# DeltaNet scan: the output of a half-step summed in PSUM on ScalarE-scaled values, with three PSUM banks for the scan and one for the preparation

## The chip, the core and the metric

The kernel runs on one core of a Trainium2 chip. The metric is the device time of one execution in microseconds (us). The kernel before was timed three times: 2514.2, 2525.34 and 2525.86 us, median 2525.34 us. A separate execution was profiled; it took 2514.53 us.

The engines are named as the profile names them: PE (TensorE; PEld is its weight load), DVE (VectorE), ACT (ScalarE), POOL (GpSimd) and SP (the queue that issues DMAs). Each runs its own list of instructions in order; they meet through semaphores only.

## What is computed

The reference is a two-layer diffusion transformer: layer 0 has a gated DeltaNet mixer in both time directions, layer 1 a gated linear attention; each is followed by a feed-forward net. The change touches the DeltaNet mixer alone. Cut to one head and one direction, a chunk does this:

```
decay = exp(where(tri, gcum_i - gcum_j, -inf))
m     = where(strict, beta_i * (k k^T) * decay, 0)
u, w  = solve(I + m, [v * beta, k * beta * exp(gcum)])
v_new = u - w @ s
o     = (q * exp(gcum)) @ s + ((q k^T) * decay) @ v_new
s     = s * exp(gcum_last) + (k * tail)^T @ v_new
```

`s` is the state that goes from chunk to chunk. There are 16 value heads in 8 groups of two, and both directions are added at the end: `o` forward plus `o` backward.

## The kernel before, in words

Tokens (256 of context, 512 of image) stand in 6 chunks of 128. The mixer is one long interleaved program. A Python loop over the groups g makes one *iteration* after another; in each it takes one step of three generators in turn: the scan `seq(g)`, the dense projections `stream()` and the side work (`advance()`).

- `stream()` gives one k-step an iteration: six matmuls of 128x128 weights against 256 and 512 columns. A projection is 8 k-steps and lands in a PSUM bank `d` for 512 columns and a half bank for 256. When it ends, ScalarE copies it out (`rp`), and a convolution of five taps runs on VectorE (`cv`, `tn`).
- `prep(g)` prepares a group: `dec` makes the decay factors E in a PSUM bank (PE, then exponentials on ACT); the products of K with K and with Q go to another bank; VectorE builds N and A; then VectorE eliminates 32x32 blocks in a loop of 30 steps (`tmp`, `X`), transposes the result (`Z`), and PE multiplies the blocks together (`ZM`, `LC`), which gives Y. One group's preparation is made while the scan of an earlier one runs.
- `seq(g)` is the scan: 12 half-steps h, direction d = h % 2, chunk c = order[d][h // 2]. A half-step takes three iterations. In the first, PE multiplies K and Q with the state S into one bank, here called **p1** (256 columns K·S, 256 columns Q·S, line 737); VectorE makes R from K·S (line 742); then `kx` ends the half-step before. Two iterations later PE multiplies U with R into a second bank, **p2** (line 758), and ScalarE copies that to x (`xv`, line 760). `kx` (line 702), called in the next half-step, multiplies x with Kt into p2's first half (from which VectorE updates S, line 717) and with A into p2's second half, which VectorE subtracts from the output oN (line 723).
- The share of Q·S in the output goes from p1 to oN separately: in a half-step that is the first to reach its chunk, ScalarE writes it scaled (line 748); otherwise VectorE multiplies and adds it (line 750).
- `onorm(g)` normalises the output after the scan. It ends with transposes on PE into the one bank `n` and a multiply on VectorE from it (`of`), four times, with one iteration between them (line 802).

PSUM has 8 banks. `psm(tag)` (line 111) hands them out: two `d`, one for the half-width outputs, one `n`, two `c` (the preparation) and two `s` (p1 and p2 of the scan, the K products, and the 256-column half of every second z projection). A new tile of a tag waits on PE until its bank has been read. The order of the matmuls that the generators issue is pinned to the program; the other engines' instructions are placed by a scheduler at compile time. Everything after the mixer (output projection, feed-forward, layer 1) is dense work that the change does not touch.

Of the kernel before, what the change touches and what calls it, by code (L numbers as in the profile page):

```python
# [8 lines left out]
F32 = mybir.dt.float32  # L9
# [6 lines left out]
P = 128  # L16
# [3 lines left out]
NCH = 6  # L20
# [40 lines left out]
class Dev:  # L61
# [8 lines left out]
    def nm(self, s):  # L70
        self.n += 1
        return f"{s}{self.n}"
# [4 lines left out]
    def stt(self, o, a, s, b, op0, op1):  # L77
        self.dve.scalar_tensor_tensor(o, a, s, b, op0=op0, op1=op1)  # L78
# [6 lines left out]
def body(tc, I, O):  # L85
# [3 lines left out]
    with ExitStack() as top:  # L89
# [21 lines left out]
        def psm(tag="c"):  # L111
            if PS["nc"] == 4 and PS["pair"] is None:
                tag = "c"
            return PS["c"].tile([P, 512], F32, name=nm(tag), tag=tag, bufs={"c": PS["nc"], "n": 1, "s": 2}[tag])

# [170 lines left out]
        with ExitStack() as dn:  # L286
            ps_scope(dn, True, 2)
            dc = dn.enter_context(tc.tile_pool(reuse_waits="tile", name="dc", bufs=1))

            RA = dc.tile([P, NT], F32R, name="RA")  # L290
            biasE = dc.tile([P, NCH, 2, 16], F32, name="biasE")
            neG = dc.tile([P, NCH, 2, 16], F32, name="neG")
            tailb = dc.tile([P, NCH, 2, 16], F32, name="tailb")
            eGl = dc.tile([P, NCH, 2, 16], F32, name="eGl")

            with tc.tile_pool(reuse_waits="tile", name="x0", bufs=1) as x0p, tc.tile_pool(reuse_waits="tile", name="n3", bufs=3) as n3:
# [37 lines left out]
            nc.sync.dma_start(convw, I["convw"])  # L334
            dve.tensor_scalar(dng, dng, -0.5, None, op0=MUL)

            with tc.tile_pool(reuse_waits="tile", name="gt", bufs=1) as gt:
# [34 lines left out]
                tt(biasE, Lb, Gc, SUB)  # L372
                act.activation(neG, Gc, AF.Exp)
                dve.tensor_scalar(neG, neG, -1.0, None, op0=MUL)
                ps = psm("n")
# [49 lines left out]
            def conv(ft, outs, bite, done):  # L425
                rp = rps[0]
                act.copy(rp[:, 2:258], outs[0])  # L427
                act.copy(rp[:, 260:772], outs[1])
                state["evac"] += 1
                cv = cv3.tile([P, NG], F32, name=nm("cv"), tag="c3")  # L430
                w = convw[:, ft]
                act.activation(cv, rp[:, 2:772], AF.Copy, scale=w[:, 2:3])  # L432
                yield
                for n, tap in enumerate((0, 1, 3, 4)):
                    stt(cv, rp[:, tap:tap + NG], w[:, tap:tap + 1], cv, MUL, ADD)
                    if n % bite == bite - 1:
                        yield
                t = cv3.tile([P, NG], F32, name=nm("tn"), tag="c3")
                act.activation(t, cv, AF.Tanh, scale=0.5)
                yield  # L440
                yield from done(cv, t)
# [84 lines left out]
            def prep(g, xb):  # L526
# [4 lines left out]
                def dec(c0, hh):  # L531
                    E = ehp.tile([P, 2, 2, P], F32, name=nm("E"), tag="eh")
                    ps = psm()
                    for d in range(2):
                        r = 32 * d + 2 * g + hh
                        pmm(ps[:, d * n:(d + 1) * n], selR[:, r:r + 1].broadcast_to([P, P]), RA[:, c0 * P:c0 * P + n], stop=False)
                        pmm(ps[:, d * n:(d + 1) * n], identR, mbR[d].unsqueeze(1).broadcast_to([P, 2, P]), start=False)
                    for d in range(2):
                        for c in range(2):
                            act.activation(E[:, d, c, :], ps[:, d * n + c * P:d * n + (c + 1) * P], AF.Exp,  # L540
                                           bias=biasE[:, c0 + c, d, 2 * g + hh:2 * g + hh + 1])
                    return E
# [112 lines left out]
                for dst, t in ((Nf, 0), (Y, 1)):  # L655
                    for b6 in range(2):
                        ps = psm()
                        for p_ in range(6):
                            pmm(ps[:, p_ * 64:(p_ + 1) * 64], Nf[:, 6 * b6 + p_], LC[:, t, 6 * b6 + p_])
                        pv = ps[:, 0:384].rearrange("p (s i) -> p s i", s=6)  # L660
                        act.copy(dst[hf[0], 6 * b6:6 * b6 + 6, 64:128], pv[hf[0]])
                        act.copy(dst[hf[1], 6 * b6:6 * b6 + 6, 0:64], pv[hf[1]])
                        yield
                    yield
# [8 lines left out]
            def seq(g):  # L673
# [27 lines left out]

                def kx(h, p2, x, Kt):
                    step, d = divmod(h, 2)
# [4 lines left out]
                    for hh in range(2):  # L708
                        pmm(p2[:, 256 + hh * P:256 + (hh + 1) * P], As[c // 2][:, c % 2, 2 * d + hh, :], x[:, hh])
                    if step < 5:  # L710
# [7 lines left out]
                    if not done[c]:  # L718
                        done[c] = True
                        if step == 0:  # L720
                            act.activation(oN[:, c], h2(p2[:, 256:512]), AF.Copy, scale=-1.0)
                            return
                    tt(oN[:, c], oN[:, c], h2(p2[:, 256:512]), SUB)

                nx = pre(0)
                prev = None
                for h in range(12):
                    step, d = divmod(h, 2)
                    c = order[d][step]
                    ks = slice(cg(c), cg(c) + P)  # L730
                    U, Kt = nx
                    if step == 0:
                        R = Vn[:, c]
                    else:
                        p1 = psm("s")
                        pmm(p1[:, 0:256], KT[:, ks], S[d])
                        pmm(p1[:, 256:512], QT[:, ks], S[d])
                        R = sp.tile([P, 2, P], F32, name=nm("R"), tag="R", bufs=1)
                        for hh in range(2):
                            stt(R[:, hh], p1[:, hh * P:(hh + 1) * P], neG[:, c, d, r0 + hh:r0 + hh + 1], Vn[:, c, hh], MUL, ADD)  # L740
                    if prev is not None:
                        kx(*prev)
                    if step > 0:
                        for hh in range(2):
                            pq = p1[:, 256 + hh * P:256 + (hh + 1) * P]
                            sg = neG[:, c, d, r0 + hh:r0 + hh + 1]
                            if not done[c]:
                                act.activation(oN[:, c, hh], pq, AF.Copy, scale=sg)
                            else:
                                stt(oN[:, c, hh], pq, sg, oN[:, c, hh], MUL, ADD)  # L750
                    if h == 11:
# [7 lines left out]
                    x = sp.tile([P, 2, P], F32, name=nm("xv"), tag="xv", bufs=1)  # L759
                    act.copy(x, h2(p2[:, 0:256]))  # L760
                    prev = (h, p2, x, Kt)
                    yield
# [3 lines left out]
            def onorm(g):  # L766
# [29 lines left out]
                for hh in range(2):  # L796
# [4 lines left out]
                    for c0, cn in ((0, 4), (4, 2)):  # L801
                        yield
                        ps = psm("n")
# [508 lines left out]
```

## Time and profile before

| | |
|---|---|
| profiled execution | 2514.53 us, of which the span from first to last instruction is 2512.8 us |
| median of three runs | 2525.34 us (2514.2 to 2525.86) |
| busy in the span | PE 91%, PEld 78%, DVE 63%, ACT 44%, POOL 39% |
| mean granted TensorE clock | 0.954 |
| scans of the 8 groups | first U matmuls at 219.5, 335.1, 467.5, 587.8, 702.2, 819.3, 934.3 and 1033.7 us |

The mixer's interleaved part lies between about 70 and 1110 us. What stands before is the first norm and the modulation weights; what follows to 2512.8 us is dense. The busy shares are means over all of it, so what the change is worth must be read from the stretches between 207 and 1110 us.

### The profile page before, as it was taken

What the parts mean: (1) busy time and instruction counts of PE and PEld (TensorE: products, weight loads), DVE (VectorE), ACT (ScalarE), POOL (GpSimd) and SP (SyncE); (2) the same over time, 40 slices, a digit from 0 to 9 for tenths busy, and PEclk for the clock granted to TensorE, in tenths of its full rate; (3) what the DMA queues carried; (4) which work ended last, traced back from release to release, by engine and by line L of the source; (5) the groups of instructions that cost most, each with busy time, mean ns of one, the idle gap of its engine ahead of it and who ended that gap; (6) DMA issues with size and microseconds to landing.
All of it is one profiled execution on the core that took longest, in us unless ns stands there. A gap on an engine that the chain in (4) does not pass through costs nothing. (4 is left out here: it accounts for less than half of the span.)

```text
span 2512.8 us, 35426 instructions
## 1 busy us (share of the span) xinstructions
PE 2282.8 (91%) x13112; PEld 1956.0 (78%) x13112; DVE 1576.4 (63%) x2655; ACT 1097.9 (44%) x2097; POOL 970.2 (39%) x908
## 2 busy tenths in 40 slices
PE   5878989898989897996899999999799999899999
PEld 3767878787878786885788888888688777688887
DVE  6488586869797978439878787872475654311111
ACT  5444545354636363532441414133475644433432
POOL 1235453435353544534233333333242334244443
PEclk8889998899999998997999999999899999899999
DMA  6111111101010111256243333331111124133332
GB/s 238 52 59 43 43 60 42 49 28 39 30 39 31 37 43 37 87 177 224 71 131 123 124 129 125 127 124 57 40 47 38 51 76 130 51 97 97 97 98 99
DMA packets 107309, 206.63 MB, mean 82 GB/s; under 512 B 12032, under 2 KB 12544, under 8 KB 107136
## 3 DMA queue, kind: packets, MB, share of 16 engines
q1 hardware_dynamic: 106848, 203.31, 24.7%
q8 instruction: 104, 1.70, 0.3%
q10 hardware_dynamic: 288, 1.05, 0.2%
q14 instruction: 69, 0.57, 0.1%
HBM read 190.68 MB, written 13.63 MB: 81 GB/s over the span
## 5 line engine op out<-in xcount | busy, mean ns | idle before, releaser
L75 POOL TENSOR_TENSOR wl<-wr,wh 128x512 fp32r<-128x512 f32 x419 | 574.0, 1371 | 994.3 <-ACT wh L204 916.7
L204 ACT CAST wh<-wr 128x512 fp32r<-128x512 f32 x452 | 279.2, 620 | 745.2 <-PE d L98 618.4
L98 PE MATMUL d<-hh,wh 128*128 128x256 f32 (+1 forms) x1088 | 339.0, 364 | 14.9 <-ACT hh L261 14.2
L98 PE MATMUL d<-hh,wl 128*128 128x256 f32 (+1 forms) x1088 | 335.5, 360 | 5.5 <-POOL wl L75 5.5
L98 PE MATMUL d<-hl,wh 128*128 128x256 f32 (+1 forms) x1088 | 335.3, 361 | 1.0 <-DVE hl L263 1.0
L75 DVE TENSOR_TENSOR avp<-avw,cB 128x512 f32<-128x512 f32 x256 | 216.0, 870 | 99.6 <-DMA avw<-ada_t 97.2
L98 PEld LDWEIGHTS d<-hh,wh 128*128 128x128 f32 x1088 | 207.2, 192 | 50.5 <-ACT hh L261 18.7
L98 PEld LDWEIGHTS d<-hh,wl 128*128 128x128 f32 x1088 | 206.6, 191 | 36.4 <-POOL wl L75 6.5
L98 PEld LDWEIGHTS d<-hl,wh 128*128 128x128 f32 x1088 | 207.2, 191 | 33.4 <-DVE hl L263 3.0
L98 PE MATMUL d<-gl,wh 128*128 128x512 f32 (+1 forms) x768 | 230.6, 355 | 0.8 <-DVE gl L75 0.8
L98 PE MATMUL d<-gh,wh 128*128 128x512 f32 (+1 forms) x768 | 230.4, 354 | 0.0
L98 PE MATMUL d<-gh,wl 128*128 128x512 f32 (+1 forms) x768 | 229.6, 353 | 0.0
L405 PE MATMUL d<-hh,wh 128*128 128x256 f32 (+1 forms) x704 | 217.7, 384 | 10.3 <-ACT rp L427 10.3
L78 DVE SCALAR_TENSOR_TENSOR xT<-d,mods,xT 128x256 f32<-128x256 f32 (+1 forms) x120 | 75.7, 656 | 200.4 <-PE d L98 200.4
L405 PE MATMUL d<-hh,wl 128*128 128x256 f32 (+1 forms) x704 | 196.7, 355 | 0.0
L405 PE MATMUL d<-hl,wh 128*128 128x256 f32 (+1 forms) x704 | 196.6, 354 | 0.0
L78 DVE SCALAR_TENSOR_TENSOR cv<-rp,convw,cv 128x770 f32<-128x770 f32 x128 | 150.7, 1177 | 25.5 <-ACT cv L432 24.9
L98 PEld LDWEIGHTS d<-gl,wh 128*128 128x128 f32 x768 | 144.1, 188 | 22.8 <-DVE gl L75 1.8
L699 POOL TENSOR_SCALAR Kt<-Kn,tb 128x128 f32<-128x128 f32 x160 | 114.0, 725 | 121.1 <-PE s L405 66.6
L98 PEld LDWEIGHTS d<-gh,wl 128*128 128x128 f32 x768 | 144.4, 188 | 20.9
L98 PEld LDWEIGHTS d<-gh,wh 128*128 128x128 f32 x768 | 144.3, 188 | 20.5
L189 DVE TENSOR_REDUCE mods<-avp 128x1 f32<-128x1024 f32 x128 | 156.0, 1218 | 3.9
(302 smaller groups left out, 4504.2 us busy)
## 6 DMA issues: line engine op xcount, KB each, us to landing
wr<-ffn SPq DMA_DIRECT2D x256, 256.0 KB, 2.7
avw<-ada_t SPq DMA_DIRECT2D x128, 256.0 KB, 3.3
aw<-ada_w SPq DMA_DIRECT2D x64, 256.0 KB, 4.7
wr<-dn_qkv SPq DMA_DIRECT2D x64, 256.0 KB, 2.8
wr<-dn_z SPq DMA_DIRECT2D x32, 256.0 KB, 2.7
wr<-dn_wo SPq DMA_DIRECT2D x32, 256.0 KB, 2.9
oD<-of SPq DMA_DIRECT2D x16, 384.0 KB, 2.3
ol<-oD SPq DMA_DIRECT2D x16, 384.0 KB, 3.8
```

Of the source, the lines that this page charges most:

```text
L75: (eng or self.dve).tensor_tensor(o, a, b, op=op)
L78: self.dve.scalar_tensor_tensor(o, a, s, b, op0=op0, op1=op1)
L98: pe.matmul(out, lhsT, rhs, start=start, stop=stop, skip_group_check=True)
L189: dve.reduce_sum(mods[:, l, part, m, s:s + 1], p, axis=mybir.AxisListType.X)
L204: act.copy(wh, r)
L405: pin(pe.matmul(out, lhsT, rhs, start=start, stop=stop, skip_group_check=True))
L699: pool.tensor_scalar(Kt[:, hh], Kn[:, c], tb[:, c, d, hh:hh + 1], None, op0=MUL)
```

## The change

In the diff below, the sign of the output is turned (x is now copied out negated, and R with its sign), so that both shares of the output have the same sign and can be added in PSUM. ScalarE scales the Q·S half of p1 in place by eG = exp(gcum); A·x of the same half-step is then accumulated by PE on top of it in p1, and one instruction moves the sum to oN: a copy on ScalarE in the half-step that is first at its chunk, an addition on VectorE otherwise. So p1 lives until the `kx` of its half-step, one half-step longer. The ring `s` has three banks in place of two and `c` one in place of two; half of the `dec` tiles and of the last block products move from `c` to `s`. Between the four transposes of `onorm` there are two iterations in place of one. (The lines with `dve.scalar_tensor_tensor` in `conv` are the same instruction, written out.)

```diff
-            return PS["c"].tile([P, 512], F32, name=nm(tag), tag=tag, bufs={"c": PS["nc"], "n": 1, "s": 2}[tag])
+            return PS["c"].tile([P, 512], F32, name=nm(tag), tag=tag, bufs={"c": PS["nc"], "n": 1, "s": 3}[tag])
...
-            ps_scope(dn, True, 2)
+            ps_scope(dn, True, 1)
...
-            dve.tensor_scalar(dng, dng, -0.5, None, op0=MUL)
+            dve.tensor_scalar(dng, dng, 0.5, None, op0=MUL)
...
-                act.activation(neG, Gc, AF.Exp)
-                dve.tensor_scalar(neG, neG, -1.0, None, op0=MUL)
+                act.activation(eG, Gc, AF.Exp)
...
                 def dec(c0, hh):
-                    ps = psm()
+                    ps = psm("s" if hh else "c")
...
                     for b6 in range(2):
-                        ps = psm()
+                        ps = psm("s" if b6 else "c")
...
-                def kx(h, p2, x, Kt):
+                def kx(h, p1, p2, x, Kt):
...
                     for hh in range(2):
-                        pmm(p2[:, 256 + hh * P:256 + (hh + 1) * P], As[c // 2][:, c % 2, 2 * d + hh, :], x[:, hh])
+                        pmm(p1[:, 256 + hh * P:256 + (hh + 1) * P], As[c // 2][:, c % 2, 2 * d + hh, :], x[:, hh], start=step == 0)
...
                     if not done[c]:
                         done[c] = True
-                        if step == 0:
-                            act.activation(oN[:, c], h2(p2[:, 256:512]), AF.Copy, scale=-1.0)
-                            return
-                    tt(oN[:, c], oN[:, c], h2(p2[:, 256:512]), SUB)
+                        act.copy(oN[:, c], h2(p1[:, 256:512]))
+                    else:
+                        tt(oN[:, c], oN[:, c], h2(p1[:, 256:512]), ADD)
...
+                    p1 = psm("s")
                     if step == 0:
                         R = Vn[:, c]
                     else:
-                        p1 = psm("s")
                         pmm(p1[:, 0:256], KT[:, ks], S[d])
-                        pmm(p1[:, 256:512], QT[:, ks], S[d])
+                        pmm(p1[:, 256:512], QT[:, ks], S[d], start=False)
                         R = sp.tile([P, 2, P], F32, name=nm("R"), tag="R", bufs=1)
                         for hh in range(2):
-                            stt(R[:, hh], p1[:, hh * P:(hh + 1) * P], neG[:, c, d, r0 + hh:r0 + hh + 1], Vn[:, c, hh], MUL, ADD)
+                            stt(R[:, hh], p1[:, hh * P:(hh + 1) * P], eG[:, c, d, r0 + hh:r0 + hh + 1], Vn[:, c, hh], MUL, SUB)
+                        for hh in range(2):
+                            pq = p1[:, 256 + hh * P:256 + (hh + 1) * P]
+                            act.activation(pq, pq, AF.Copy, scale=eG[:, c, d, r0 + hh:r0 + hh + 1])
                     if prev is not None:
                         kx(*prev)
-                    if step > 0:
-                        for hh in range(2):
-                            pq = p1[:, 256 + hh * P:256 + (hh + 1) * P]
-                            sg = neG[:, c, d, r0 + hh:r0 + hh + 1]
-                            if not done[c]:
-                                act.activation(oN[:, c, hh], pq, AF.Copy, scale=sg)
-                            else:
-                                stt(oN[:, c, hh], pq, sg, oN[:, c, hh], MUL, ADD)
...
-                    act.copy(x, h2(p2[:, 0:256]))
-                    prev = (h, p2, x, Kt)
+                    act.activation(x, h2(p2[:, 0:256]), AF.Copy, scale=1.0 if step == 0 else -1.0)
+                    prev = (h, p1, p2, x, Kt)
...
                     for c0, cn in ((0, 4), (4, 2)):
-                        yield
+                        yield from idle(2)
                         ps = psm("n")
```

The change moves instructions on three engines. Names below are tiles with their numbers; a number is given anew by each build, so that the same tile has another one in the changed kernel.

VectorE, scan of the fifth group (output oN1211 before), from the R of one half-step to just past the R of the next; `cv` and `tn` are the convolution, `tmp` and `X` the elimination. Before:

```order
L78 SCALAR_TENSOR_TENSOR R1255_6678<-s1254_6675,neG_96,Vn1066_5698 128x128 x2
L78 SCALAR_TENSOR_TENSOR S1228_6565<-S1228_6565,eGl_98,s1247_6653 128x128 x2
L75 TENSOR_TENSOR oN1211_6498<-oN1211_6498,s1247_6653 128x256
L78 SCALAR_TENSOR_TENSOR oN1211_6498<-s1254_6675,neG_96,oN1211_6498 128x128 x2
L78 SCALAR_TENSOR_TENSOR cv1245_6648<-rp0_618,convw_549,cv1245_6648 128x770
L75 TENSOR_TENSOR tmp1293_6869<-X1220_6526 128x238
L78 SCALAR_TENSOR_TENSOR cv1245_6648<-rp0_618,convw_549,cv1245_6648 128x770
L75 TENSOR_TENSOR X1220_6526<-X1220_6526,tmp1293_6869 128x17x14
L78 SCALAR_TENSOR_TENSOR cv1245_6648<-rp0_618,convw_549,cv1245_6648 128x770
L78 SCALAR_TENSOR_TENSOR R1264_6733<-s1263_6730,neG_96,Vn1066_5698 128x128 x2
L78 SCALAR_TENSOR_TENSOR S1241_6621<-S1241_6621,eGl_98,s1260_6715 128x128 x2
L75 TENSOR_TENSOR oN1211_6498<-oN1211_6498,s1260_6715 128x256
```

The same half-steps in the changed kernel (oN1220 there):

```order
L78 SCALAR_TENSOR_TENSOR R1266_6690<-s1265_6687,eG_98,Vn1080_5721 128x128 x2
L78 SCALAR_TENSOR_TENSOR S1239_6577<-S1239_6577,eGl_97,s1258_6665 128x128 x2
L75 TENSOR_TENSOR oN1220_6509<-oN1220_6509,s1250_6623 128x256
L434 SCALAR_TENSOR_TENSOR cv1256_6660<-rp0_617,convw_549,cv1256_6660 128x770
L75 TENSOR_TENSOR X1219_6507<-X1219_6507,tmp1292_6838 128x16x15
L434 SCALAR_TENSOR_TENSOR cv1256_6660<-rp0_617,convw_549,cv1256_6660 128x770
L75 TENSOR_TENSOR tmp1300_6861<-X1219_6507 128x238
L434 SCALAR_TENSOR_TENSOR cv1256_6660<-rp0_617,convw_549,cv1256_6660 128x770
L78 SCALAR_TENSOR_TENSOR R1275_6745<-s1274_6742,eG_98,Vn1080_5721 128x128 x2
L78 SCALAR_TENSOR_TENSOR S1252_6635<-S1252_6635,eGl_97,s1271_6727 128x128 x2
L75 TENSOR_TENSOR oN1220_6509<-oN1220_6509,s1265_6687 128x256
```

The two oN instructions that read p1 (s1254) are gone, and the oN addition that is left reads p1 of the half-step before (s1250, s1265) where it read p2.

ScalarE, the same half-steps; `xv` is x, `wh` the cast of dense weights. Before:

```order
L760 COPY xv1261_6718<-s1260_6715 128x256
L204 CAST wh1266_6747<-wr1265_6745 128x512
L439 ACTIVATE tn1268_6757<-cv1245_6648 128x770
L748 ACTIVATE oN1211_6498<-s1263_6730,neG_96 128x128 x2
L760 COPY xv1274_6780<-s1273_6777 128x256
L748 ACTIVATE oN1211_6498<-s1276_6791,neG_96 128x128 x2
```

In the changed kernel, with the evacuation `rp` that follows:

```order
L741 ACTIVATE s1265_6687<-s1265_6687,eG_98 128x128 x2
L753 ACTIVATE xv1272_6730<-s1271_6727 128x256
L204 CAST wh1277_6759<-wr1276_6757 128x512
L438 ACTIVATE tn1279_6769<-cv1256_6660 128x770
L741 ACTIVATE s1274_6742<-s1274_6742,eG_98 128x128 x2
L753 ACTIVATE xv1285_6792<-s1284_6789 128x256
L719 COPY oN1220_6509<-s1274_6742 128x256
L741 ACTIVATE s1287_6803<-s1287_6803,eG_98 128x128 x2
L426 COPY rp0_617<-d2561224_6516 128x256
```

A pair of scalings stands in every half-step from h = 2 on, where before it stood at h = 4 to 7 only (and wrote oN); the copy to oN is an instruction of its own.

PE, the preparation between the scans of the fourth and the fifth group: the last block products of one group (`LC`) meet the decay factors (`RA`) and the K products (`KT`) of the next. Before:

```order
L405 MATMUL c1178_6280<-LC_620,N934_4970 128x64 x6
L405 MATMUL c1180_6290<-RA_94,cR_545 128x256
L405 MATMUL c1180_6290<-cR_545,identR_73 128x256
L405 MATMUL c1180_6290<-RA_94,cR_545 128x256
L405 MATMUL c1180_6290<-cR_545,identR_73 128x256
L405 MATMUL s1181_6299<-KT1144_6082 128x128
```

In the changed kernel:

```order
L404 MATMUL s1187_6292<-LC_619,N940_4975 128x64 x6
L404 MATMUL s1189_6302<-RA_94,cR_545 128x256
L404 MATMUL s1189_6302<-cR_545,identR_73 128x256
L404 MATMUL s1189_6302<-RA_94,cR_545 128x256
L404 MATMUL s1189_6302<-cR_545,identR_73 128x256
L404 MATMUL s1190_6311<-KT1148_6068 128x128
```

The order is the same and the banks are not: all three tiles are of the ring `s` now, of which the running z projection holds one bank, so that the K products take the bank that the block products have just filled.

## Rows read from the trace of the kernel before

**Rows 1.** The page's first part: busy time, share of the span, instructions of each engine.
```profile
PE 2282.8 (91%) x13112; PEld 1956.0 (78%) x13112; DVE 1576.4 (63%) x2655; ACT 1097.9 (44%) x2097; POOL 970.2 (39%) x908
```

**Rows 2.** Busy us by stretch (PE, PEld, DVE, ACT, POOL, clock, DMA): seven eliminations, one and sum.
```profile
701.00:755.00 54.00, 46.40 (x288) 40.23 (x288) 49.62 (x105) 19.33 (x48) 30.23 (x32) 1.00 0.13 42
...
sum 370.00, PE 320.04 PEld 276.82 DVE 346.64 ACT 131.02 POOL 209.80; mean PE 45.72 PEld 39.55 DVE 49.52 ACT 18.72 POOL 29.97
```

**Rows 3.** The same view of the eight stretches between and behind them, one and sum.
```profile
640.00:701.00 61.00, 54.96 (x375) 49.76 (x376) 45.73 (x92) 39.70 (x86) 25.89 (x30) 0.97 0.09 29
...
sum 533.00, PE 481.04 PEld 433.87 DVE 327.35 ACT 303.50 POOL 213.16; mean PE 60.13 PEld 54.23 DVE 40.92 ACT 37.94 POOL 26.64
```

**Rows 4.** Waits of PE, 210 to 1110 us: us in total, times, longest.
```profile
PE s L405 <- DVE oN L75: 27.6, 14, 4.9
PE n L805 <- DVE of L78: 22.4, 12, 3.4
PE s L405 <- ACT oN L748: 15.8, 12, 3.3
PE s L405 <- DVE oN L78: 6.2, 6, 1.3
PE s L405 <- DVE R L78: 4.9, 4, 2.6
PE d L405 <- ACT rp L427: 4.1, 14, 0.8
```

**Rows 5.** Timeline of VectorE, 719 to 722 us: start, length, what.
```profile
719.07 1.01 DVE L78 SCALAR_TENSOR_TENSOR cv<-rp,convw,cv 128x770 f32<-128x770 f32 x1
720.00 0.59 DVE L78 SCALAR_TENSOR_TENSOR R<-s,neG,Vn 128x128 f32<-128x128 f32 x2
720.52 0.59 DVE L78 SCALAR_TENSOR_TENSOR S<-S,eGl,s 128x128 f32<-128x128 f32 x2
721.04 0.41 DVE L75 TENSOR_TENSOR oN<-oN,s 128x256 f32<-128x256 f32 x1
721.37 0.60 DVE L78 SCALAR_TENSOR_TENSOR oN<-s,neG,oN 128x128 f32<-128x128 f32 x2
```

**Rows 6.** Timeline of PE there, with the idle time ahead of the row.
```profile
721.59 0.68 PE L405 MATMUL s<-R,U 128*128 128x128 f32 x4 [1.43 <-DVE oN L75]
```

**Rows 7.** The instructions on tile oN: durations in ns, min/median/max.
```profile
L78 DVE SCALAR_TENSOR_TENSOR oN<-s,neG,oN x96: 271/341/407, 234.7 to 1092.0; 128x128 f32<-128x128 f32 x96
L75 DVE TENSOR_TENSOR oN<-oN,s x80: 402/410/483, 240.3 to 1095.4; 128x256 f32<-128x256 f32 x80
L748 ACT ACTIVATE oN<-s,neG x64: 348/360/370, 251.8 to 1070.0; 128x128 f32<-128x128 f32 x64
L721 ACT ACTIVATE oN<-s x16: 387/391/393, 223.0 to 1041.9; 128x256 f32<-128x256 f32 x16
```

**Rows 8.** Busy us on oN alone within one elimination: DVE, then ACT.
```profile
701.00:755.00 54.00, 3.17 (x9) 3.26 (x10) 1.00 0.13 42
```

**Rows 9.** Timeline of PE: first and last wait for oN outside the eliminations.
```profile
252.53 1.20 PE L405 MATMUL s<-R,U 128*128 128x128 f32 x4 [3.25 <-ACT oN L748]
...
1003.99 0.68 PE L405 MATMUL s<-R,U 128*128 128x128 f32 x4 [0.68 <-DVE oN L75]
```

**Rows 10.** Timeline between two scans: block products and decay factors on PE, copies on ACT.
```profile
561.59 1.45 PE L405 MATMUL c<-LC,N 128*128 128x64 f32 x12
...
563.05 0.28 PE L405 MATMUL c<-cR,identR 128*128 128x256 f32 x1
...
563.07 0.47 ACT L661 COPY N<-c 64x384 f32<-64x384 f32 x1 [0.96 <-PE c L405]
565.10 0.47 ACT L662 COPY N<-c 64x384 f32<-64x384 f32 x1
```

**Rows 11.** Waits of ACT, 210 to 1110 us.
```profile
ACT xv L760 <- PE s L405: 131.2, 69, 7.4
ACT oN L748 <- DVE R L78: 53.1, 22, 3.6
```

More of the change, by code (lines that the diff above doesn't have):

```diff
@@ L291, in body @@
             biasE = dc.tile([P, NCH, 2, 16], F32, name="biasE")
-            neG = dc.tile([P, NCH, 2, 16], F32, name="neG")
             tailb = dc.tile([P, NCH, 2, 16], F32, name="tailb")
             eGl = dc.tile([P, NCH, 2, 16], F32, name="eGl")
+            eG = dc.tile([P, NCH, 2, 16], F32, name="eG")
             with tc.tile_pool(reuse_waits="tile", name="x0", bufs=1) as x0p, tc.tile_pool(reuse_waits="tile", name="n3", bufs=3) as n3:
@@ L434, in conv @@
                 for n, tap in enumerate((0, 1, 3, 4)):
-                    stt(cv, rp[:, tap:tap + NG], w[:, tap:tap + 1], cv, MUL, ADD)
+                    dve.scalar_tensor_tensor(cv, rp[:, tap:tap + NG], w[:, tap:tap + 1], cv, op0=MUL, op1=ADD)
                     if n % bite == bite - 1:
```

## The prediction

> **What bounds the kernel now.** I read the busy shares of the page first: PE 91%, VectorE 63% [rows 1]. That mean covers some 1400 us of dense work that the change leaves alone, so the next view is the busy time by stretch between 207 and 1110 us. It falls into two kinds. In the seven stretches in which VectorE eliminates the blocks of the next group while the scan runs, 370 us in all, VectorE is busy 346.6 us (94%) and PE only 320.0 (86%) [rows 2]: here PE runs at VectorE's pace. In the other stretches, 533 us, VectorE is busy 327.4 us (61%) and PE 481.0 (90%) [rows 3]. PE thus stands idle 50 us in the first kind and 52 us in the second.
>
> The waits say what for [rows 4]. PE waits 27.6 + 15.8 + 6.2 = 49.6 us for oN, on VectorE and on ScalarE: no matmul reads oN, it is the bank that oN's instructions have yet to read. It waits 22.4 us for `of`, the readout's single bank, and 4.9 us for R itself. One such wait in close-up: VectorE finishes R at 720.59, S at 721.11, the oN addition at 721.45 [rows 5], and p2's matmul starts at 721.59, after 1.43 us of idleness that began at 720.16 [rows 6]. So 0.43 us of it is R being late, 0.52 is S, and 0.34 with the signal is oN. R is late because a convolution step (1.01 us) stands ahead of it [rows 5]. The bank is the smaller part of the wait; VectorE's list is the larger.
>
> **What goes from VectorE.** Of the output instructions, 96 multiply-adds of 128x128 and 32 of the 80 additions of 128x256 go. A pair of the former takes 0.60 us [rows 5], 0.30 each, and an addition 0.41 [rows 7]: 28.8 + 13.1 = 42 us over eight groups. What that is worth depends on the stretch. In one elimination nine oN instructions run, 3.17 us [rows 8]: four multiply-adds and five additions, of which two additions stay (the two half-steps that reach a chunk second). 4 x 0.30 + 3 x 0.41 = 2.4 us, times seven is 17 us. VectorE sets the pace there, so I count it in full, and count nothing extra for the earlier release of the banks in the same stretches, since PE would only run ahead and wait for R.
>
> Outside them eleven waits for oN make 24.2 us of the 49.6 (the first and the last of them [rows 9]). p2 now waits mostly for S in place of the oN addition. Bounds: 0.33 us each (start of the addition to start of what follows it [rows 5]), 3.6 us in all, if R stays as late; 24.2 if all goes. I take 8, a third, near the lower end, since by the close-up R and S are most of a wait.
>
> **What goes with two iterations between the readout's transposes.** An iteration holds at least a k-step, so the `of` multiply gets more than twice the time before PE wants the bank. Bounds are 0 (VectorE is still behind, and the wait passes to the next R) and 22.4 us [rows 4]. I take 17: these waits lie outside the eliminations, where VectorE has slack [rows 3].
>
> **What ScalarE gets.** 160 scalings in place and 48 copies, less 64 scalings and 16 copies to oN. By the nearest rows (0.36 and 0.39 us [rows 7]) this is 96 x 0.36 + 32 x 0.39 = 47 us more. The trace has no ScalarE write to PSUM; I bound a scaling between 0.27 (below its SBUF form by a quarter) and 0.41 (VectorE's addition, [rows 7]), which is 43 to 65 us of scalings, and take 0.36. It stays at 131 + 304 = 435 us of 903 [rows 2, 3] plus 47, so 53%. The sum is needed by A·x three iterations later, behind two k-steps: I cost it at nothing on PE's path, with x delayed by up to one scaling. That x feeds `kx` only after the next k-step, which hides it. For the scalings standing ahead of casts and evacuations I charge 4 us.
>
> **The rings.** The scan's third bank is what lets p1 live on; without it p2 would wait for the previous sum. The preparation has the same four banks, since the z projection holds one, but in the order shown the K products follow the block products into one bank. They wait for two copies of 0.47 us [rows 10] less the four decay matmuls between (0.28 us or less each, overlapping), so some 0.6 us with the signal. I count two such places in each of six groups: 7 us lost. Bounds: 0, if the ring finds another bank free, and 14. The first norm's second matmul moves behind some weights for want of a second `c` bank: under 1 us, not counted.
>
> **Sum.** 17 + 8 + 17 - 4 - 7 = 31 us. From the profiled execution, 2514.5, that is 2483.5. The median of the three runs lies 10.8 above the profiled execution and their lowest run at its height; I add a third of the difference and say 2487.
>
> **The rivals.**
> - *Everything goes.* Both waits vanish and nothing follows: 49.6 + 22.4 - 7 = 65 us, 2450. For it: VectorE is slack in 533 of the 903 us. Against it: 94% busy in the eliminations, where 2.4 us less in 54 can't repay 5 us of waits. Chance 0.19.
> - *The wait is handed on.* R comes no earlier: VectorE's list is filled up with elimination steps, and S takes oN's place. Then 32 waits [rows 4] give 0.33 each, 11 us, the readout's wait passes to R, and the preparation loses 7: 2510, between 2503 and 2518. For it: the close-up. Against it: the elimination is as long as before, so what is filled in ends sooner. Chance 0.18.
> - *Slower: ScalarE is held.* A scaling can start only when R has been read: the 22 waits of the old scaling for R took 53.1 us, 2.4 each [rows 11]. There were 32 such pairs, now there are 80, and in the new order 24 of the 33 convolution evacuations stand within four rows behind one, where 11 did. If each of these 24 is held 2.4 us and PE waits for its bank `d`, 58 us are lost: 2483.5 + 58 = 2541. It decides from about half that price on. For it: the order. Against it: ScalarE already stands 131.2 us for x [rows 11], which comes after the same R, so the hold replaces that wait; and PE's wait for evacuations is only 4.1 us now [rows 4]. Chance 0.11.
>
> The waits of old oN scalings for R [rows 11] show the hold that this rival rests on. The Trainium skill states the rule behind it ("PSUM — Partial Sum Buffer", section "PSUM bank collisions raise a hardware error"): two engines that touch one bank must be kept apart by a semaphore on the bank, even where they touch different columns. By it no other half of p1 would help, and the trace agrees, since R and the scaling read different halves; without it ScalarE would scale while VectorE reads, and this rival would have no chance.
>
> **How the numbers follow.** The forecast has 0.52. Its own range, from the bounds of the unknown costs (8 by 3.6 or 15, 17 by 8 or 22, 7 by 0 or 14, 4 by 0 or 12), is 2466 to 2506, not all ends at once. With half of the first rival left below and the slow one above, 2455 to 2519 leaves out about 0.2. A difference of 0.5% (12.6 us) is about what a measurement can tell here. Faster than 2512.7: 0.52 + 0.19 + 0.07 (the lower part of the handed-on wait) = 0.78. Within 0.5%: 0.11 of that rival and 0.02 of a half-paid slow one, 0.13. Slower: 0.09.
>
> **What would show it.** Right: PE's waits for `of` fall under 6 us; p2 waits for S or R where it waited for oN, with 2 to 3 us less in each elimination, which shrinks from 54 to about 51 us; VectorE's busy time falls by about 40 us and ScalarE's rises by about 50. Wrong: eliminations of the same length (handed on); under 48 us (everything goes); waits of PE for `rp` or the casts of tens of us (ScalarE held); new waits of the K products well over 14 us.

## The result and the profile after

The changed kernel is slower: 2554.06 us, median of four runs (2544.05 to 2562.42), beside 2523.28 us for the kernel before; the ratio is 1.0127, with a 95% interval of 1.0081 to 1.0173, some 32 us. The prediction was 2487 us. The profiled execution took 2556.61 us, 42.1 more than that of before. Its page begins so (busy time, share of the span, instructions; compare [rows 1]):

```profile
PE 2317.1 (91%) x13112; PEld 1980.6 (78%) x13112; DVE 1551.4 (61%) x2526; ACT 1138.8 (45%) x2225; POOL 971.2 (38%) x908
```

The same 13112 matmuls took 34.3 us longer, and PE's idle time (span less busy) grew by 7.8 us only. So most of the loss is matmuls that took longer, not waiting: the mean granted clock fell from 0.954 to 0.945 over the span. VectorE's busy time fell by 25.0 us where about 40 were forecast, ScalarE's rose by 40.9. The waits of PE, 210 to 1140 us (us in total, times, longest; compare [rows 4]), have changed altogether:

```profile
PE d L404 <- ACT rp L426: 26.9, 17, 3.6
PE s L404 <- DVE S L78: 12.2, 13, 2.4
PE n L798 <- DVE of L78: 10.9, 13, 1.3
PE c L404 <- ACT Y L646: 10.7, 5, 2.4
PE s L404 <- ACT xv L753: 8.1, 11, 2.4
...
PE s L404 <- DVE R L78: 4.5, 2, 2.5
...
PE n L404 <- DVE of L78: 3.3, 1, 3.3
...
PE s L404 <- ACT N L661: 2.0, 4, 1.0
```

The 49.6 us for oN are gone, as forecast, and 16.7 for S and R stand in their place. The wait for `of` fell from 22.4 to 14.2 (10.9 and 3.3). New or longer are `rp` (4.1 before), Y on the preparation's single bank, and xv. The last row holds the waits for which the prediction charged the rings 7 us: of its 2.0 us, three waits of 1.0 us in all stand ahead of K products.

**Ahead of the first scan.** The first scan starts at 228.8 us; before it started at 219.5. The last stretch ahead of it holds 222 matmuls in both kernels. Busy time by stretch (columns as [rows 2]), first of before, then of after:

```profile
186.00:219.50 33.50, 31.04 (x222) 28.12 (x223) 26.98 (x59) 21.94 (x49) 15.21 (x20) 0.95 0.13 40
```

```profile
187.20:228.80 41.60, 36.61 (x222) 33.62 (x223) 26.40 (x64) 21.98 (x49) 15.83 (x20) 0.79 0.10 32
```

PE's timeline of after shows two new waits on the one bank `c`, for the copies of Y:

```profile
196.13 0.58 PE L404 MATMUL c<-RA,cR 128*128 128x256 f32 x1 [2.00 <-ACT Y L630]
210.20 0.99 PE L404 MATMUL c<-LC,N 128*128 128x64 f32 x7 [2.42 <-ACT Y L646]
```

They are 4.4 us. The stretch is 8.1 longer: PE is idle 2.5 us more, and the same matmuls take 5.6 us more, at a mean granted clock of 0.79 in place of 0.95, a mix of the two levels 1.2 and 2.4 GHz. The same happens between later scans. After one wait of 2.12 us for Y, at 694.8 us, the changed kernel does 60 matmuls in the 14 us that follow, at 0.51:

```profile
697.00:711.00 14.00, 13.91 (x60) 13.19 (x61) 4.17 (x10) 7.26 (x16) 1.99 (x2) 0.51 0.07 19
```

In experiment 4 below the same wait is 0.76 us, and the next 14 us hold 99 matmuls at the full clock:

```profile
694.60:708.60 14.00, 12.93 (x99) 12.25 (x100) 9.59 (x23) 8.77 (x26) 6.54 (x8) 1.00 0.12 39
```

A section of the Trainium skill ("TensorE: Matmul & The Clock Gate", "A second HAM failure mode: psum-queue depth-cycling") says that a kernel that cycles through PSUM banks can leave PE idle for moments so often that its clock goes up and down, at a loss of throughput. The traces agree on the loss, here behind single waits of 2.0 to 2.4 us: 222 matmuls took 33.5 us at 0.95 and 41.6 us at 0.79.

**In the scan.** ScalarE waits in front of its scalings (its waits in the changed kernel, 210 to 1140 us):

```profile
ACT s L741 <- DVE R L78: 124.7, 57, 5.2
ACT xv L753 <- PE s L404: 57.0, 45, 5.8
```

In close-up, VectorE, ScalarE and PE of the changed kernel around one of PE's waits for `rp`:

```profile
619.51 0.60 DVE L78 SCALAR_TENSOR_TENSOR R<-s,eG,Vn 128x128 f32<-128x128 f32 x2
```

```profile
620.24 0.72 ACT L741 ACTIVATE s<-s,eG 128x128 f32<-128x128 f32 x2 [4.69 <-DVE R L78]
620.88 0.61 ACT L204 CAST wh<-wr 128x512 fp32r<-128x512 f32 x1
621.38 0.38 ACT L426 COPY rp<-d 128x256 f32<-128x256 f32 x1
```

```profile
621.81 1.00 PE L404 MATMUL d<-hh,wh 128*128 128x256 f32 x2 [2.83 <-ACT rp L426]
```

ScalarE stood still for 4.69 us because R came at 619.51, behind several elimination steps, and the copy that PE needed stood two places behind the scaling.

### The profile page after: what moved, and what is told of

It is laid out like the page before. It is cut to its first block, busy times and chain, and to the rows that moved or that the text cites. A ratio compares the mean times of both kernels' runs of the same rounds, so it can differ in the third digit from the quotient of the medians.

```text
span 2554.9 us, 35301 instructions
## 1 busy us (share of the span) xinstructions
PE 2317.1 (91%) x13112; PEld 1980.6 (78%) x13112; DVE 1551.4 (61%) x2526; ACT 1138.8 (45%) x2225; POOL 971.2 (38%) x908
## 5 line engine op out<-in xcount | busy, mean ns | idle before, releaser
L98 PE MATMUL d<-hh,wh 128*128 128x256 f32 (+1 forms) x1088 | 340.4, 366 | 15.0 <-ACT hh L261 14.3
L75 DVE TENSOR_TENSOR avp<-avw,cB 128x512 f32<-128x512 f32 x256 | 236.4, 953 | 84.8 <-DMA avw<-ada_t 82.5
L404 PE MATMUL d<-hh,wh 128*128 128x256 f32 (+1 forms) x704 | 222.5, 392 | 33.4 <-ACT rp L426 33.1
L98 PEld LDWEIGHTS d<-hh,wh 128*128 128x128 f32 x1088 | 207.2, 192 | 51.1 <-ACT hh L261 18.2
L434 DVE SCALAR_TENSOR_TENSOR cv<-rp,convw,cv 128x770 f32<-128x770 f32 x128 | 144.9, 1132 | 33.0 <-ACT cv L431 31.9
L404 PEld LDWEIGHTS d<-hh,wh 128*128 128x128 f32 x704 | 125.1, 204 | 45.5 <-ACT rp L426 38.9
```

The source lines that it names most:

```text
L75: (eng or self.dve).tensor_tensor(o, a, b, op=op)
L98: pe.matmul(out, lhsT, rhs, start=start, stop=stop, skip_group_check=True)
L404: pin(pe.matmul(out, lhsT, rhs, start=start, stop=stop, skip_group_check=True))
L434: dve.scalar_tensor_tensor(cv, rp[:, tap:tap + NG], w[:, tap:tap + 1], cv, op0=MUL, op1=ADD)
```

## The experiments

Theory A was that ScalarE is held by its scalings, theory B that the preparation's single bank costs the time. Ratios are against the kernel before, with 95% intervals. In the diffs, `...` stands for lines and arguments that are not shown.

**1. The rings alone.** Kernel before with:
```diff
-... bufs={"c": PS["nc"], "n": 1, "s": 2}[tag])
+... bufs={"c": PS["nc"], "n": 1, "s": 3}[tag])
...
-            ps_scope(dn, True, 2)
+            ps_scope(dn, True, 1)
...
                 def dec(c0, hh):
...
-                    ps = psm()
+                    ps = psm("s" if hh else "c")
...
                     for b6 in range(2):
-                        ps = psm()
+                        ps = psm("s" if b6 else "c")
```


> The kernel before with the change of the rings alone: three banks for the scan and one for the preparation, half of the decay tiles and of the last block products in the scan's ring. Arithmetic and instructions as before. Theory A (ScalarE is held by scalings that wait for R, and the evacuations rp stand behind them) expects the rings to cost little: PE's waits for oN (49.6 us before) fall under 10 us because the third bank takes them, waits for rp stay under 6 us, time between 0.985 and 1.003 of before. Theory B (the preparation's single bank is what costs: block products wait for the copies of Y, PE idles there and the clock falls) expects PE's waits for Y and N on the ring c of 10 us or more, and 1.005 to 1.015 of before.

1.0044 (1.0027 to 1.0062): B's sign, at its lower edge. The first scan starts at 229.1 us, 9.6 later than before, and that is nearly all of the 11 us. PE's waits:

```profile
PE s L405 <- DVE R L78: 33.4, 26, 4.7
PE n L805 <- DVE of L78: 23.2, 13, 3.4
PE d L405 <- ACT rp L427: 12.5, 15, 2.2
PE c L405 <- ACT Y L647: 7.5, 6, 2.4
...
PE s L405 <- DVE oN L75: 3.9, 3, 2.4
```

With a third bank the wait for oN is nearly gone, and most of it stands for R instead (33.4 us, where 4.9 stood before): R was late all the time, the bank hid it.

**2. Scalings behind x.** Changed kernel with:
```diff
-                        for hh in range(2):
-                            pq = p1[:, 256 + hh * P:256 + (hh + 1) * P]
-                            act.activation(pq, pq, AF.Copy, scale=eG[...])
                     if prev is not None:
                         kx(*prev)
...
                     act.activation(x, h2(p2[:, 0:256]), AF.Copy, ...)
+                    if step > 0:
+                        for hh in range(2):
+                            pq = p1[:, 256 + hh * P:256 + (hh + 1) * P]
+                            pin(act.activation(pq, pq, AF.Copy, scale=eG[...]))
```


> The changed kernel with one edit: the two scalings of a half-step are pinned on ScalarE's list right behind the copy x of the same half-step, so that ScalarE no longer waits for R in front of them (x needs R anyway). Theory A expects PE's waits for rp to fall from 26.9 us to under 8 us, ScalarE's waits in front of the scalings from 119.7 us to under 10 us, and a time of 0.985 to 1.000 of the kernel before (25 to 60 us under the changed kernel). Theory B expects the waits for Y (12.8 us) and the low clock between the scans to stay and the time to stay at 1.007 or above.

1.0062 (1.0040 to 1.0084). Waits for `rp` halve to 13.5 us, but A·x now waits 18.2 us for the scaling. This is above theory A's range and below theory B's; with the first run it says that both have a part.

**3. Two iterations between the transposes, alone.** Kernel before with:
```diff
-                        yield
+                        yield from idle(2)
                         ps = psm("n")
```


> The kernel before with two iterations instead of one between the transposes of the output norm, nothing else. The prediction's step on the wait for of expects these waits to fall from 22.4 us to under 8 us and the time to 0.990 to 0.996 of before (10 to 25 us). The rival (the wait passes to the next R) expects 0.998 to 1.002, with the waits of PE for oN or R longer by as much.

1.0003 (0.9986 to 1.0021). The wait for `of` fell as the changed kernel's did, and the time did not. PE's idle time is 5.3 us less than before and its matmuls take 6.0 us more ([rows 1] and the first line below). PE's waits follow (the rows for oN, `of` and Vn):

```profile
PE 2288.8 (91%) x13112; PEld 1958.1 (78%) x13112; DVE 1583.5 (63%) x2655; ACT 1097.3 (44%) x2097; POOL 974.8 (39%) x908
```

```profile
PE s L405 <- DVE oN L75: 25.5, 15, 3.5
PE s L405 <- ACT oN L748: 13.6, 12, 3.3
PE n L805 <- DVE of L78: 11.0, 11, 2.7
...
PE n L516 <- ACT Vn L421: 4.4, 1, 4.4
...
PE n L405 <- ACT Vn L421: 3.6, 2, 2.6
...
PE n L405 <- DVE of L78: 3.3, 1, 3.3
```

**4. One iteration again.** Changed kernel with:
```diff
-                        yield from idle(2)
+                        yield
                         ps = psm("n")
```


> The changed kernel with one iteration between the transposes again, as before. If the two iterations are worth something in the changed kernel, it is slower than the changed kernel: waits for of 20 us or more and 1.016 to 1.022 of the kernel before. If what they save passes to another wait, 1.010 to 1.015, as the changed kernel itself (1.0127).

1.0101 (1.0082 to 1.0121), if anything better than the changed kernel: the two iterations gain nothing there either. The intervals overlap.

**5. Other tiles in the rings.** Experiment 1 with:
```diff
-                ps = psm()
+                ps = psm("s" if state["sfree"] else "c")
                 for p_ in range(12):
                     pmm(ps[:, p_ * 32:(p_ + 1) * 32], Y[:, p_], ZM[:, p_])
...
-                        ps = psm("s" if b6 else "c")
+                        ps = psm("c" if b6 else "s")
```


> The kernel before with the rings changed (three banks for the scan, one for the preparation) but other tiles in them: the first block product ZM x Y stands in the scan's ring where no scan runs, and of the two last block products it is the first that does. Theory B1 (nearly all of the rings' cost arises ahead of the first scan, where two waits for Y on the single bank let the clock fall: the first scan starts at 229 us with the changed rings in every kernel so far, at 219.5 to 220.2 us with two banks for the preparation) expects the two waits of 2.0 and 2.4 us to go, a start at 219 to 222 us and 0.998 to 1.002 of before. The rival (the cost is spread over all groups) expects a start of 226 us or later or, with an early start, still 1.003 to 1.006.

1.0008 (0.9990 to 1.0025): the loss of the rings is gone, as far as the interval tells. Of the two waits for Y ahead of the first scan one is gone and one is 0.62 us, and the stretch with the 222 matmuls is

```profile
186.00:223.90 37.90, 34.17 (x222) 31.13 (x223) 27.19 (x59) 21.96 (x49) 15.26 (x20) 0.86 0.12 36
```

The scan starts at 223.9, between the two kernels, a little later than expected. Over all the profiles the first scan starts at 219.5 and 220.2 us with two banks for the preparation (before and experiment 3), at 228.8 to 230.5 with one bank and the change's tiles (six kernels), and at 221.0 to 226.3 with one bank and these tiles (six kernels).

**6. Scalings ahead of p2.** Changed kernel, the scalings pinned where p2 is issued:
```diff
-                        for hh in range(2):
-                            pq = p1[:, 256 + hh * P:256 + (hh + 1) * P]
-                            act.activation(pq, pq, AF.Copy, scale=eG[...])
...
                     yield
+                    if step > 0:
+                        for hh in range(2):
+                            pq = p1[:, 256 + hh * P:256 + (hh + 1) * P]
+                            pin(act.activation(pq, pq, AF.Copy, scale=eG[...]))
                     p2 = psm("s")
```


> The changed kernel with the two scalings issued two iterations later, right ahead of p2, and pinned on ScalarE's list behind what was issued on it before. Theory A (ScalarE's list is held where a scaling waits for R) expects ScalarE's waits for R under 40 us (119.7 in the changed kernel), PE's waits for rp under 15 us (26.9), and almost no waits of A x for the scaling (18.1 us with the scaling behind x), so 1.000 to 1.005 of before. The rival (what is freed passes to R and S anyway, the sum in PSUM brings nothing) expects 1.005 to 1.009, as with the scaling behind x.

1.0106 (1.0079 to 1.0133). ScalarE's waits for R fell to 53.4 us and PE's for `rp` to 13.2, and little time came of it (5 us, within the intervals): theory A's size is wrong.

**7. All three.** Experiment 6 with the edit of experiment 5 and that of experiment 4:
```diff
-                ps = psm()
+                ps = psm("s" if state["sfree"] else "c")
...
-                        ps = psm("s" if b6 else "c")
+                        ps = psm("c" if b6 else "s")
...
-                        yield from idle(2)
+                        yield
```


> The changed kernel with the later scalings, the other tiles in the rings, and one iteration between the transposes. If the hold of ScalarE and the waits ahead of the first scan are all that the changed kernel loses, what is left is the work taken from VectorE: 0.990 to 0.998 of before, with a first start at 219 to 222 us. The rival (the wait for R sets the scan's pace, whoever reads it) expects 0.999 to 1.004.

0.9997 (0.9980 to 1.0014): the whole loss is undone, and nothing is won that is clear of the noise, beside the kernel before or beside experiment 5 (1.0008), which has the same rings and sums nothing in PSUM. VectorE is busy 42.8 us less than before. The first scan starts at 226.3 us, later than the expected 219 to 222.

**8. The hold alone.** Experiment 1 with:
```diff
+                        if done[c]:
+                            for hh in range(2):
+                                act.activation(p1[:, hh * P:(hh + 1) * P], p1[:, 256 + hh * P:256 + (hh + 1) * P], AF.Copy, scale=neG[...])
```


> The kernel before with the changed rings, and with ScalarE scalings added in the half-steps that have none: each writes its result over the K S half of p1 once R has read it, where nothing reads it, so that only ScalarE's wait for R and 96 instructions are added; VectorE keeps its work. Theory A expects PE's waits for rp of 20 us or more (12.5 with the rings alone) and 1.008 to 1.013 of before (1.0044 with the rings alone). The rival (the hold costs nothing, since ScalarE waits for x after the same R) expects 1.003 to 1.006.

1.0063 (1.0044 to 1.0082) beside 1.0044: a price of about 5 us, though the intervals overlap; PE's waits for `rp` are 17.1 us. Nearer to the rival. The kernel does 64 scalings more, not the 96 of the expectation: `done[c]` is read ahead of the `kx` that sets it for the half-step before, so that h = 2 and h = 8 got none.

**9. The other tiles in the changed kernel.** The edit of experiment 5 on the changed kernel:
```diff
-                ps = psm()
+                ps = psm("s" if state["sfree"] else "c")
...
-                        ps = psm("s" if b6 else "c")
+                        ps = psm("c" if b6 else "s")
```


> The changed kernel with the other tiles in the rings alone (first block product in the scan's ring where no scan runs, of the last two products the first there); scalings and the two iterations between the transposes as in the changed kernel (1.0127). If the preparation's single bank is the main loss, 1.000 to 1.005 of before, with waits for Y on it under 4 us (12.8). If ScalarE's hold is the main loss, 1.007 to 1.012, with waits for rp still over 20 us.

1.0053 (1.0033 to 1.0074), clear of the changed kernel's interval: the tiles that shared the single bank cost it 0.74%, 19 us. The same edit between experiments 4 and 10 gives 0.80%. PE still waits 24.9 us for `rp`. The clock came back: it is the last figure but two of these lines, for 100 to 1200 us before, in the changed kernel and here.

```profile
100.00:1200.00 1100.00, 956.23 (x6045) 845.36 (x6044) 823.74 (x1658) 513.86 (x1133) 496.41 (x528) 0.93 0.19 62
```

```profile
100.00:1200.00 1100.00, 957.01 (x5910) 845.58 (x5909) 757.59 (x1501) 547.03 (x1248) 479.13 (x518) 0.91 0.18 58
```

```profile
100.00:1200.00 1100.00, 955.83 (x5996) 843.77 (x5995) 772.44 (x1517) 551.20 (x1255) 490.70 (x525) 0.93 0.18 61
```

PE is busy as long in all three, within 1.2 us, and the changed kernel gets fewest matmuls done in it (5910 of 6045).

**10. And one iteration.** Experiment 9 with:
```diff
-                        yield from idle(2)
+                        yield
```


> As the last, and with one iteration between the transposes: all of the changed kernel but the tiles in the rings and the two iterations, that is with the scalings early on ScalarE's list. Beside the same kernel with later scalings (0.9997) it tells what the hold costs by itself: by the theory of the hold 1.004 to 1.010, by its rival (ScalarE's hold costs next to nothing once the rings are right, as the added scalings did: 1.0063 against 1.0044) 0.998 to 1.003.

1.0021 (1.0001 to 1.0040). The two iterations cost 0.3% there, as in experiment 4. Against experiment 7 the early scalings cost 0.24%, 6 us. In both pairs the intervals overlap. PE's wait for `rp`, and ScalarE's for R, here and then in experiment 7:

```profile
PE d L404 <- ACT rp L426: 23.6, 23, 2.1
```

```profile
ACT s L741 <- DVE R L78: 130.9, 49, 5.3
```

```profile
PE d L404 <- ACT rp L426: 8.6, 17, 1.7
```

```profile
ACT s L749 <- DVE R L78: 58.7, 24, 5.3
```

**11. VectorE's work put back.** Experiment 7 with:
```diff
+                        if done[c]:
+                            for hh in range(2):
+                                pk = p1[:, hh * P:(hh + 1) * P]
+                                stt(pk, pk, eG[...], Vn[:, c, hh], MUL, SUB)
```


> The kernel with later scalings, other tiles in the rings and one iteration (0.9997 of before), with VectorE's work put back: in each half-step that is not the first to reach its chunk VectorE does R's two multiply-adds a second time, into the dead half of p1, 96 instructions of 0.3 us, about 29 us. If VectorE sets the pace in the eliminations, as the prediction had it, 15 to 25 us come back: 1.005 to 1.010 of before. If the eliminations get longer and the scans still start as far apart (VectorE's time there is not on the path), 0.998 to 1.003.

1.0003 (0.9986 to 1.0020) beside 0.9997: no difference clear of the noise, and the 15 to 25 us did not come back. As in experiment 8, 64 instructions were added and not 96; VectorE is busy 24.9 us more by its page.

**12. Behind x, with the rings right.** Experiment 2 with the edits that experiment 7 adds to experiment 6:
```diff
-                ps = psm()
+                ps = psm("s" if state["sfree"] else "c")
...
-                        ps = psm("s" if b6 else "c")
+                        ps = psm("c" if b6 else "s")
...
-                        yield from idle(2)
+                        yield
```


> The changed kernel with the scalings behind x (1.0062 of before), the other tiles in the rings and one iteration between the transposes. The scalings behind x were 0.4% better than those ahead of p2 (1.0062 against 1.0106), both with the single bank as the change has it. If this stays with the rings put right, 0.993 to 0.998 of before, faster than the kernel before, with A x waiting for the scaling about as long as there (18 us). If the gain of the one over the other came from where the low clock fell, or if the waits of A x for the scaling cost what the hold cost, 0.999 to 1.004.

1.0031 (1.0014 to 1.0048), slower than experiment 7: PE waits 3.4 us for `rp`, but 18.9 for the scaling and 13.8 for xv. Why the place behind x was the better one with the single bank (1.0062 against 1.0106) and is the worse one here stays open.

## Why the prediction was wrong

Its sum was 17 + 8 + 17 - 4 - 7 = 31 us won. By the runs it is about 0 + 0 - 8 - 6 - 19 = 33 us lost, where 32 were measured. The three losses are the steps from the changed kernel over experiments 9 and 10 to experiment 7, so they add up by construction; the two zeros together are what is left there, 0.9997. Only the 19 is clear of its intervals alone. The 8 and the 6 are differences whose intervals overlap, though each has its sign in two pairs (the two iterations in experiments 4 and 10, but not on the kernel before, experiment 3; the hold in experiments 7 and 8).

- **"VectorE sets the pace there, so I count it in full" (17 us): wrong.** The eliminations did get shorter, about as worked out. First and last step of one elimination on VectorE, before, then experiment 7:

```profile
703.16 0.60 DVE L75 TENSOR_TENSOR tmp<-X 128x30 f32<-128x30 f32 x1
...
749.82 0.21 DVE L75 TENSOR_TENSOR X<-X,tmp 128x30 f32<-128x30 f32 x1
```

```profile
709.42 0.62 DVE L75 TENSOR_TENSOR tmp<-X 128x30 f32<-128x30 f32 x1
...
753.97 0.22 DVE L75 TENSOR_TENSOR X<-X,tmp 128x30 f32<-128x30 f32 x1
```

That is 46.9 us and 44.8 us, 2.1 shorter (forecast: 2.4). From first to last step the seven eliminations add up to 318.4 us before, 305.7 in the changed kernel, 295.4 in experiment 7 and 306.6 in experiment 11. But these two scans start as far apart as before. Their first matmuls, before, then experiment 7:

```profile
702.21 0.27 PE L405 MATMUL s<-Vn,U 128*128 128x128 f32 x1
...
819.25 0.27 PE L405 MATMUL s<-Vn,U 128*128 128x128 f32 x1
```

```profile
708.50 0.27 PE L404 MATMUL s<-Vn,U 128*128 128x128 f32 x1
...
826.18 0.38 PE L404 MATMUL s<-Vn,U 128*128 128x128 f32 x2
```

117.0 and 117.7 us. From the first scan's start to the eighth's it was 814.2 us before. In experiment 7, then in experiment 11, the two starts are

```profile
226.26 0.27 PE L404 MATMUL s<-Vn,U 128*128 128x128 f32 x1
...
1035.74 0.27 PE L404 MATMUL s<-Vn,U 128*128 128x128 f32 x1
```

```profile
221.03 0.27 PE L404 MATMUL s<-Vn,U 128*128 128x128 f32 x1
...
1038.83 0.38 PE L404 MATMUL s<-Vn,U 128*128 128x128 f32 x2
```

or 809.4 and 817.8 us apart. So 23.0 us less of elimination came with 4.8 us less between the scans. In experiment 11, 11.2 us more of it came with 8.4 us more, behind a first scan that starts 5.2 us earlier; the medians differ by 0.06%, 1.5 us, and their intervals leave room for some 8. A full count is not what the runs show; that a few us of VectorE's work are on the path is not excluded. My reading, which no run shows by itself, is that an engine 94% busy in a stretch [rows 2] bounds the time only if what comes next waits for the end of that stretch, and that a group as a whole is bound by PE's list. The pages of experiments 7 and 11 (spans 2513.6 and 2516.5 us):

```profile
PE 2275.7 (91%) x13112; PEld 1942.6 (77%) x13112; DVE 1533.6 (61%) x2526; ACT 1137.3 (45%) x2225; POOL 970.5 (39%) x908
```

```profile
PE 2273.2 (90%) x13112; PEld 1939.8 (77%) x13112; DVE 1558.5 (62%) x2590; ACT 1138.7 (45%) x2225; POOL 968.0 (38%) x908
```

PE's idle time is 237.9 and 243.3 us there, 230.0 before [rows 1] and 237.8 in the changed kernel; over all experiments it lies between 224.7 (experiment 3) and 245.7 us (experiment 8). A wait that goes mostly uncovers another.

- **The oN waits outside (8 us): right that R and S are most of a wait, wrong that a third would come back.** Experiment 1 leaves 33.4 us for R where 49.6 stood for oN. The rival "the wait is handed on" had this mechanism, though the sign that it named, eliminations of the same length, did not show.
- **The transposes (17 us): wrong.** The wait fell by 8 us instead of 16 or more, and even this bought nothing (experiment 3); in the changed kernel the second iteration rather costs (0.3%, within the intervals).
- **ScalarE (4 us): mechanism right, size nearly.** A scaling takes 342 ns (0.36 was taken), ScalarE's busy time rose by 41 us (47), and the hold costs about 6 us. With the single bank, scalings elsewhere gave back 5 us (experiment 6) or 16 (experiment 2), so the price depends on the rest. The slower rival told the sign and came near the time (2541), but that is luck: it gave the hold 58 us and the rings no more than 7. PE waits 22.8 us more for `rp`, as it said, but waits less elsewhere: in the close-up `rp` is late by the same R that p2 waited for before.
- **The rings (7 us, at most 14): the step that failed most.** The wait that it priced, K products behind block products, measured 1.0 us in place of 7. Of the tiles that follow one another in a bank I counted those and not the ones that wait for the copies of Y. Two things more were left out. The views began at 207 us, while the first new wait ends at 196; there was nothing in the change that spared the preparation of the first group, where no scan hides it. And the waits were priced at their length: 4.4 us of them, with the low clock behind them, made the first scan 9.3 us later. The price was 11 us by itself (experiment 1) and 19 in the changed kernel (experiment 9).

Of the 42 us between the two profiled executions, 9 lie in the dense part, which the change leaves alone (1373.6 us from its first matmul to the end, 1364.6 before); in other profiles it is between 1362.8 and 1373.8, so that need not be an effect of the change.

## What to carry to other kernels

A wait need not be worth its length, since something else can be late behind it: give the resource alone first (here a third bank) and see whose name the wait bears then. When buffers move from one ring to another, walk through every user of the ring that shrinks, the start-up phase too, and price a new wait on PE by the clock behind it as well as by its length. An engine's busy share in a stretch is no proof that its work is on the path: add or take some of that work alone, and see how much of it the time shows.

## What was not expected of the hardware

A stretch of 222 matmuls with two new waits of 2.0 and 2.4 us took 8.1 us longer, most of it by the clock (0.95 to 0.79). ScalarE's scaling in place in PSUM has a median of 342 ns, against 360 to SBUF before [rows 7]:

```profile
L741 ACT ACTIVATE s<-s,eG x160: 304/342/361, 240.9 to 1123.4; 128x128 f32<-128x128 f32 x160
```

Experiment 8 has both forms in one kernel, with the same medians:

```profile
L743 ACT ACTIVATE s<-s,neG x64: 315/342/372, 247.3 to 1109.3; 128x128 f32<-128x128 f32 x64
L751 ACT ACTIVATE oN<-s,neG x64: 342/360/368, 259.0 to 1087.3; 128x128 f32<-128x128 f32 x64
```

The Trainium skill ("ScalarE: Activation LUTs", "Step-by-step: what each stage is for") calls PSUM the faster destination for ScalarE; the traces agree, by 5% here.
